# Local attention: the rounded part of the gated outputs by a second product on Pool, and the banded blocks' queries loaded two blocks ahead

## The chip, the core and the metric

The kernel runs on one core of a Trainium2 chip. A core has five engines that each take their own instructions in order: PE (TensorE, matrix products), DVE (VectorE), ACT (ScalarE), POOL (GpSimd) and SP (SyncE, which issues most of the DMA transfers here). They wait for one another by semaphores. The metric is the device time of one execution, in microseconds (us); lower is better.

## The reference

The reference is a two-layer backbone over 2048 latent tokens (a grid of 32 rows by 64 columns) of width 1024, with 256 context tokens beside them. Each layer normalises and modulates its input, projects it, runs two branches, multiplies each branch by its own gate, and projects the concatenation back into the residual:

```python
for layer in range(DEPTH):
    h = modulated_norm(x, norm_g[layer], shift[:, None], scale[:, None])
    p = jnp.matmul(h, w_in[layer])
    if layer % 2 == 0:
        y, y_ctx = even_mixer(p, p_ctx, ...)
    else:
        y, y_ctx = odd_mixer(p, p_ctx, ...)
    x = x + gate[:, None] * jnp.matmul(y, w_out[layer])
```

The change lies mostly in the second layer's mixer, whose two branches are local attention, each with 8 query heads of 64:

```python
y_w = windowed_gqa(q_w, k_w, v_w, kc_w, vc_w, sink)
y_n = neighbourhood_attention(q_n, k_n, v_n, kc_n, vc_n, rpb)
y = jnp.concatenate([y_w * jax.nn.silu(wg), y_n * jax.nn.silu(ng)], axis=-1)
```

Both also attend to the 256 context tokens. The banded branch has a sink logit and shares its two key heads among four query heads each; the neighbourhood branch adds a learned bias (`rpb`) by relative position.

## The kernel before

Products are taken in pieces: a float is split into a rounded part `hi` (in the type fp32r) and the rest `lo = y - hi`, and a matrix product is made of several products of such parts. So whatever is to be multiplied later is stored twice, as `hi` and as `lo`.

Layer 1's local attention is one sequence of blocks of four units each. It goes over four head pairs (`hp` 0 to 3); in each pair stand four banded blocks of 128 queries by 8 heads (`w`, `window(qt)`) and then four neighbourhood blocks of 512 queries by 2 heads (`n`, `nat_block(hp, qb)`): `"wwwwnnnn"`. The banded blocks are numbered through here, w0 to w15, four to a pair. That makes 32 blocks and 128 units. A unit forms scores for two heads at a time (L1493 and L1499 on PE), a masked minimum on DVE (L1549, or L1642 to L1647 for neighbourhood blocks), exponentials on ACT (L1551, or L1644 to L1650), transposes of the probabilities on PE (L1512) whose results ACT (first head) and DVE (second head) copy to SBUF (`npT`, L1514), and the products with the values on PE (L1524).

PE's order there is written by hand as a software pipeline: step i issues the transposes of unit i+1 between the scores of unit i+3, then the values of unit i, and then the end of the block that unit i-1 closed. So the gate matmuls of a block's end stand right ahead of the first scores of the block two further on. The other engines' orders come from the scheduler's own simulated timeline, and each engine then holds to its order.

The end of a block is `attn_out`, also used by the two context blocks of layer 0, which makes 34 uses. Ahead of it `attn_norm` copies the result from PSUM to the tile `ao` on ACT (L1096; a ring of three buffers). `attn_out` loads the gate (`ggt`, L1104), broadcasts the reciprocal sums on PE (`apr`, L1108), forms gate by reciprocal on DVE (L1109), and then: POOL multiplies `ao` by the gate (L1111), ACT rounds that into `ahi` (L1113), POOL subtracts to make `alo` (L1114), and SP stores both (L1116, L1117) to `yU`, which the output projection of the layer reads after all blocks are done.

Loads: the first unit of a block has a `load`. A banded block's load is 512 KB of queries (`wq1`, L1535, a ring of two buffers) and two halves of 128 KB (`wq2`, L1538, a ring of four); in the profile both are called `wq`. A neighbourhood block loads `nq1` and `nq2` (L1614, L1617). The loop calls the load of the next block when the second unit of a block gives its scores, so queries are loaded one block ahead:

```python
if su:
    if su.k == 1 and loaded < len(firsts):
        units[firsts[loaded]].load()
        loaded += 1
```

At the start of each head pair, its keys and values (L1600 to L1606) and its bias tables are made as well. For each of the pair's two heads, three pieces of bias are loaded by SP in several small transfers each (`raw`, L1589, three buffers), and POOL subtracts each from the mask to make a part of the table `tb` (L1590). The two heads' tables are read by the neighbourhood blocks behind the pair's four banded blocks.

Of the kernel before, what the change touches and what calls it, by code (L numbers as in the profile page):

```python
# [11 lines left out]
F32R = mybir.dt.float32r  # L12
AF = mybir.ActivationFunctionType
ALU = mybir.AluOpType
# [3 lines left out]
P = 128  # L18
# [16 lines left out]
def flow_kernel(tc, I, C, out):  # L35
    nc = tc.nc
    with ExitStack() as ctx:
        kern(ctx, tc, nc, I, C, out)


def kern(ctx, tc, nc, I, C, out):
    cp = ctx.enter_context(tc.tile_pool(name="cp", bufs=1))
    dr = ctx.enter_context(tc.tile_pool(name="dr", bufs=1, space=DRAM))
    V, S, G, T = nc.vector, nc.scalar, nc.gpsimd, nc.tensor
# [198 lines left out]
    class Proj:  # L243
# [6 lines left out]
        def __init__(self, layer, rg, hp, sb, lp, ps, npt, mms):  # L250

            self.layer, self.rg, self.hp, self.sb, self.lp, self.ps, self.npt = layer, rg, hp, sb, lp, ps, npt
            self.mms = [m for m in mms for _ in range(m[2])]
            self.nm = 0
            self.junk = sb, "sq"
            self.gains = {}
# [842 lines left out]
    def attn_out(A, D, order, parts):  # L1099


        gt = A.gt("ggt")
        for sl, g, _ in parts:
            nc.sync.dma_start(gt[sl], g)  # L1104
        pr = A.t("apr")
        for u in range(8):
            c = order(u)
            T.matmul(pr[64 * (u % 2):64 * (u % 2) + 64, u // 2, :], D["den"][:, c:c + 1].to_broadcast([P, 64]), ident, start=True, stop=True, skip_group_check=True)  # L1108
        V.scalar_tensor_tensor(out=gt, in0=pr, scalar=0.5, in1=gt, op0=ALU.mult, op1=ALU.mult)  # L1109
        y = D["o"]  # L1110
        G.tensor_tensor(out=y, in0=y, in1=gt, op=ALU.mult)  # L1111
        hi, lo = A.hl("ahi", F32R), A.hl("alo", F32R)
        S.copy(hi, y)  # L1113
        G.tensor_tensor(out=lo, in0=y, in1=hi.bitcast(F32), op=ALU.subtract)  # L1114
        for sl, _, st in parts:
            nc.sync.dma_start(st(0), hi[sl].bitcast(F32))  # L1116
            nc.sync.dma_start(st(1), lo[sl].bitcast(F32))  # L1117

    def by_head(t):
        return t.rearrange("f (b d) t -> d (f b) t", b=2)  # L1120
# [40 lines left out]
    with stS as st:  # L1161
# [33 lines left out]
        with ExitStack() as s2:  # L1195
# [16 lines left out]
            aw = []  # L1212
# [212 lines left out]
    for g in range(3):  # L1425
# [9 lines left out]
        if g == 2:  # L1435
            stX.close()
            aw = stA.enter_context(tc.tile_pool(name="aw", bufs=1, **L))
# [14 lines left out]
    with ExitStack() as st:  # L1452
        sb = st.enter_context(tc.tile_pool(name="at1", bufs=1, **Rt))
        ps = st.enter_context(tc.tile_pool(name="ats1", bufs=1, space=PSUM, **Rt))
        A = K()
# [19 lines left out]
        def probs():  # L1475
            return sb.tile([P, 896], F32, tag="np", name="np", bufs=7)

        class Unit:


            def __init__(self, B, k, qk, cols, kts, soft):
                self.B, self.k, self.qk, self.cols, self.kts, self.soft = B, k, qk, cols, kts, soft
                self.load = self.end = self.S_then = self.V_then = None
                self.last = False

            def scores(self):

# [41 lines left out]
        def window(qt):  # L1529
            tok = slice(qt * P, qt * P + P)  # L1530
            B = {"v": lambda: wvt}

            def load():
                q1 = aw.tile([P, 8, P], F32R, tag="wq1", name="wq1", bufs=2)
                nc.sync.dma_start(q1.bitcast(F32), qk1[0:8, :, tok].rearrange("h p t -> p h t"))  # L1535
                q2 = A.q2("wq2", F32R)
                for s in range(2):
                    nc.sync.dma_start(q2[64 * s:64 * s + 64].bitcast(F32), qk1[4 * s:4 * s + 4, 0:64, tok].rearrange("h p t -> p h t"))  # L1538
                B["q"] = q1, q2
                B["den"] = sb.tile([P, 8], F32, tag="gden", name="gden", bufs=3)  # L1540
                B["mx"] = sb.tile([P, 8], F32, tag="gmx", name="gmx", bufs=3)

            lo, hi = max(qt - 1, 0), min(qt + 1, 15)
            nl = (hi - lo + 1) * P
            m = wm[:, 640:1152] if qt == 0 else wm[:, 0:256 + nl]

            def soft(g, kv, s):
                h, p, mx, den = 4 * kv + g, probs(), B["mx"], B["den"]
                V.tensor_tensor_reduce(out=p[:, :256 + nl], in0=s[:, 256:512 + nl], in1=m, scale=1.0, scalar=sk[:, h:h + 1],  # L1549
                                       op0=ALU.add, op1=ALU.min, accum_out=mx[:, h:h + 1])  # L1550
                S.activation(p[:, :256 + nl], p[:, :256 + nl], AF.Exp, bias=mx[:, h:h + 1], scale=-1.0, accum_out=den[:, h:h + 1])  # L1551
                if g == 3 and kv == 1:
                    es = sb.tile([P, 8], F32, tag="ges", name="ges", bufs=2)
                    V.tensor_tensor(out=es, in0=mx, in1=sk, op=ALU.subtract)
                    S.activation(es, es, AF.Exp)
                    V.tensor_tensor(out=den, in0=den, in1=es, op=ALU.add)
                return p

            def end():
                store = [lambda t, kv=kv: by_head(yU[t, 0:4])[:, 4 * kv:4 * kv + 4, tok] for kv in range(2)]  # L1560
                attn_out(A, B, lambda u: 4 * (u % 2) + u // 2, [(slice(64 * kv, 64 * kv + 64), by_head(g1[0:4])[:, 4 * kv:4 * kv + 4, tok], store[kv]) for kv in range(2)])

            def qk(g):
                q1, q2 = B["q"]
                return lambda kv: q1[:, 4 * kv + g, :], q2[:, g, :], wk1, wk2

            us = [Unit(B, g, lambda g=g: qk(g), [(256, 2048, 256, True), (512, lo * P, nl, True)], [16, 17] + list(range(lo, hi + 1)),
                       lambda kv, s, g=g: soft(g, kv, s)) for g in range(4)]
            us[0].load, us[3].end = load, end
            return us  # L1570

# [22 lines left out]
        def nat_keys(hp):  # L1594
            hs = slice(18 + 2 * hp, 20 + 2 * hp)
            k1 = sb.tile([P, 2, 2304], F32R, tag="nk1", name="nk1", bufs=1)
            k2 = sb.tile([P, 2304], F32R, tag="nk2", name="nk2", bufs=1)
            for s in range(2):
                r = slice(64 * s, 64 * s + 64)
                nc.sync.dma_start(k1[r].bitcast(F32), qk1[hs, 0:64].rearrange("h p t -> p h t"))  # L1600
                nc.sync.dma_start(k2[r].bitcast(F32), qk1[18 + 2 * hp + s, 64:P])
            heads["k", hp] = k1, k2

        def nat_values(hp):
            heads["v", hp] = vt = sb.tile([P, 18, P], F32, tag="nv", name="nv", bufs=1)
            nc.sync.dma_start(vt, v1n[:, :, hp * P:(hp + 1) * P].rearrange("t p d -> p t d"))  # L1606
# [74 lines left out]
        units, qt = [], 0  # L1681
        for hp in range(4):
            qb = 0
            for i, what in enumerate("wwwwnnnn"):
                if what == "w":
                    units += window(qt)
                    units[-1].last = qt == 15
                    qt += 1
                    if i < 2:
                        units[-1].S_then = (lambda hp=hp: nat_tables(hp)) if i else lambda hp=hp: nat_keys(hp)  # L1690
                    continue
                us = nat_block(hp, qb)
                qb += 1
                if qb == 4 and hp < 3:
                    us[3].V_then = lambda hp=hp: nat_values(hp + 1)
                units += us
        n = len(units)
        firsts = [i for i, u in enumerate(units) if u.load]
        units[firsts[0]].load()
        nat_values(0)  # L1700
        loaded = 1
        with tc.manual_schedule(engines={mybir.EngineType.PE}):
            for i in range(-3, n + 1):
                su = units[i + 3] if i + 3 < n else None
                sc = su.scores() if su else [None] * 3
                tr = units[i + 1].transposes() if 0 <= i + 1 < n else []
                tr += [None] * (4 - len(tr))
                for f in (tr[0], sc[0], tr[1], sc[1], tr[2], sc[2], tr[3]):
                    if f:
                        f()  # L1710
                if su:
                    if su.k == 1 and loaded < len(firsts):
                        units[firsts[loaded]].load()
                        loaded += 1
                    if su.S_then:
                        su.S_then()
                if 0 <= i < n:
                    units[i].values()
                    if units[i].V_then:
                        units[i].V_then()  # L1720
                if 0 <= i - 1 < n and units[i - 1].end:
                    units[i - 1].end()
                    if units[i - 1].last:
                        prepare()
# [182 lines left out]
```

## Time and profile before

| | |
|---|---|
| median of three runs | 4063.99 us (4061.94 to 4068.01) |
| profiled execution | 4068.84 us |
| its span on the core | 4067.10 us |
| mean clock granted to PE | 0.954 of full speed |
| PE, busy share of the span | 91% |
| DVE | 61% |
| ACT | 44% |
| POOL | 41% |

The profile is one execution, recorded instruction by instruction. A row of the timeline gives the start in us from the span's beginning, the length in us, the engine, the line of the kernel, the operation and the tiles it writes and reads; brackets behind it hold the time for which the engine stood idle ahead of the row, and what ended that time. The waits group such idle times by who waited at which line for whom. The chain of waits follows the work that ended last back from the end of a stretch. A row of the table by stretches gives busy time of each engine with its count of instructions, the clock granted to PE (PEclk, 1.00 is full speed), the mean busy share of the DMA engines and the GB/s moved. A group of instructions is shown with its count, its busy time and the mean of one in ns, and then the idle time ahead of its rows.

The layer-1 local attention runs from about 3230 to 3890 us of the span.

### The profile page before, as it was taken

Reading aid. Unit: us, or ns where it says so; the run is one execution under the profiler, and the core shown is the slowest. Engines: PE = TensorE matmul, PEld = TensorE weight load, DVE = VectorE, ACT = ScalarE, POOL = GpSimd, SP = SyncE. Lnnn points to the kernel's source line nnn. Section 1 sums busy time; section 2 is a strip of 40 time slices with the busy share of each in tenths; the row PEclk is TensorE's granted clock in tenths of the full one; section 3 lists DMA queues with packets and bytes.
Section 4 is the critical chain, followed back from the end, with each engine's and each line's share of the span. In section 5 each row is a group of like instructions: output and inputs, shape, how many; then the busy total and the mean of one; then the engine's idle time right before and its main releaser. Section 6 shows DMA issues by size and latency. Waiting matters only on the chain.

```text
span 4067.1 us, 57048 instructions
## 1 busy us (share of the span) xinstructions
PE 3687.4 (91%) x20080; PEld 2634.0 (65%) x20080; DVE 2475.5 (61%) x4464; ACT 1794.6 (44%) x3460; POOL 1669.6 (41%) x1420
## 2 busy tenths in 40 slices
PE   6799889998959988899988989999998999989999
PEld 2588767656734443444444647777877877877887
DVE  6754852627769875688775528377158166666632
ACT  4554643425435543455443334343233265665610
POOL 1544542221456665576666555443344211121210
PEclk9899989999969998999998999999999999999999
DMA  6443445465474433343325435465466366265455
GB/s 189 102 137 120 131 121 139 126 240 186 141 211 130 134 115 134 95 136 122 96 103 174 127 109 162 144 178 155 131 192 162 118 161 140 82 145 126 121 156 173
DMA packets 525825, 576.14 MB, mean 142 GB/s; under 512 B 70790, under 2 KB 361920, under 8 KB 521442
## 3 DMA queue, kind: packets, MB, share of 16 engines
q1 hardware_dynamic: 516834, 547.25, 46.2%
q0 software_dynamic: 8704, 25.24, 1.6%
q8 instruction: 158, 2.59, 0.3%
q14 instruction: 129, 1.06, 0.1%
HBM read 383.73 MB, written 188.57 MB: 141 GB/s over the span
## 4 chain that ended last, share of the span: by engine, by line
PE 32%; DVE 6%; DMA 5%; issue 4%; POOL 2%; ACT 2%; SPq 1%; ACTq 0%; POOLq 0%; DVEq 0%
PE pso L215 7%; PE psB L215 4%; PE npt L1512 4%; PE no L1524 3%; PE psA L215 3%; PE po L950 2%; PE ns L1493 2%; DMA raw<-rpb 2%; PE ns L1499 1%; DMA wraw<-in_w_in_dram 1%; PE pS L929 1%; POOL wlo L237 1%; PE pS L930 1%; PE pm L887 1%; DMA wraw<-in_w_out_dram 1%
## 5 line engine op out<-in xcount | busy, mean ns | idle before, releaser
L237 POOL TENSOR_TENSOR wlo<-wraw,whi 128x512 fp32r<-128x512 f32 x368 | 488.5, 1343 | 872.3 <-ACT whi L236 600.2
L942 POOL TENSOR_TENSOR pacc<-pacc,Pt 128x512 f32<-128x512 f32 x448 | 609.0, 1378 | 314.4 <-ACT Pt L931 311.6
L215 PE MATMUL psB<-hT,whi 128*128 128x512 f32 (+1 forms) x2560 | 662.1, 348 | 19.6 <-DVE bo L333 7.4
L215 PE MATMUL psA<-whi,hT 128*128 128x512 f32 (+1 forms) x1952 | 569.9, 373 | 22.7 <-DVE hT L301 6.9
L931 ACT ACTIVATE Pt<-pS 128x512 f32<-128x512 f32 x576 | 336.0, 598 | 407.4 <-PE pS L930 396.4
L215 PEld LDWEIGHTS psB<-hT,whi 128*128 128x128 f32 x2560 | 447.1, 192 | 98.6 <-issue 16.5
L888 DVE TENSOR_REDUCE mx<-pm 128x1 f32<-128x512 f32 (+1 forms) x640 | 388.1, 630 | 151.6 <-PE pm L887 148.9
L215 PE MATMUL psB<-hT,wlo 128*128 128x512 f32 (+1 forms) x1280 | 438.6, 348 | 2.6 <-POOL wlo L237 2.5
L215 PEld LDWEIGHTS psA<-whi,hT 128*128 128x128 f32 x1952 | 355.7, 193 | 91.4 <-DVE hT L301 10.4
L215 PE MATMUL pso<-whi,oy 128*128 128x512 f32 x1088 | 346.5, 397 | 18.6 <-DMA oy<-yT 10.5
L215 PE MATMUL psA<-wlo,hT 128*128 128x512 f32 (+1 forms) x976 | 355.3, 369 | 1.3 <-POOL wlo L237 1.2
L929 PE MATMUL pS<-Q,K 128*128 128x512 f32 x576 | 341.2, 592 | 6.1 <-ACT Pt L931 5.7
L236 ACT CAST whi<-wraw 128x512 fp32r<-128x512 f32 x368 | 221.9, 618 | 268.3 <-DMA wraw<-in_w_in_dram 131.6
L887 PE MATMUL pm<-K,Q 128*128 128x512 f32 (+1 forms) x640 | 252.4, 422 | 77.3 <-DVE mx L888 58.1
L950 PE MATMUL po<-Pt,V 128*64 128x512 f32 x1152 | 291.8, 629 | 0.0
L1512 PE MATMUL npt<-ident,np 128*128 128x128 f32 x1488 | 262.2, 286 | 27.5 <-ACT npT L1514 25.5
L215 PEld LDWEIGHTS psB<-hT,wlo 128*128 128x128 f32 x1280 | 244.1, 191 | 39.0 <-POOL wlo L237 5.5
L215 PEld LDWEIGHTS pso<-whi,oy 128*128 128x128 f32 x1088 | 207.0, 191 | 71.0 <-ACT whi L236 9.9
L929 PEld LDWEIGHTS pS<-Q,K 128*128 128x128 f32 x576 | 114.2, 198 | 206.7 <-issue 145.6
L930 PE MATMUL pS<-Q,K 65*128 65x512 f32 x576 | 239.2, 415 | 6.2 <-DMA Q<-mr 6.2
L887 PEld LDWEIGHTS pm<-K,Q 128*128 128x128 f32 x640 | 133.2, 208 | 134.3 <-DVE mx L888 86.9
L1512 PEld LDWEIGHTS npt<-ident,np 128*128 128x128 f32 x1488 | 172.1, 142 | 73.4 <-ACT npT L1514 35.6
(334 smaller groups left out, 6784.4 us busy)
## 6 DMA issues: line engine op xcount, KB each, us to landing
wraw<-in_w_in_dram SPq DMA_DIRECT2D x312, 256.0 KB
oy<-yT SPq DMA_DIRECT2D x72, 512.0 KB
qk<-tq SPq DMA_DIRECT2D x68, 512.0 KB
fA<-fev SPq DMA_DIRECT2D x64, 256.0 KB
hxb<-XA SPq DMA_DIRECT2D x64, 256.0 KB
hfb<-fA SPq DMA_DIRECT2D x64, 256.0 KB
XC<-hevc POOLq DMA_DIRECT2D x64, 256.0 KB, 2.4
hdi<-XC SPq DMA_DIRECT2D x64, 256.0 KB
```

The lines of the kernel that those rows point to most:

```text
L215: T.matmul(ps, a(x, kt), b(y, kt), start=(kt == 0 and n == 0), stop=(kt == 7 and n == 2))
L236: S.copy(hi, w)
L237: G.tensor_tensor(out=lo, in0=w, in1=hi.bitcast(F32), op=ALU.subtract)
L887: T.matmul(pm[:, :n], q1[:, h, qt * P:(qt + 1) * P], K1[hp // 2][:, c0:c0 + n], start=True, stop=True)
L888: V.tensor_reduce(out=mx[:, u, c:c + 1], in_=pm[:, :n], axis=AX.X, op=ALU.max)
L929: T.matmul(s, K1[kv][:, kt * P:(kt + 1) * P], q1[:, h, :], start=True, stop=False)
L930: T.matmul(s, K2[kv][:, kt * P:(kt + 1) * P], q2[:, h, :], start=False, stop=True)
L931: S.activation(pt[:, h, :], s, AF.Exp)
L942: (G if e else V).tensor_tensor(out=acc[e][:, h], in0=acc[e][:, h], in1=p[:, h], op=ALU.add)
L950: T.matmul(po[64 * h:64 * h + 64, :], vt[:, kt, kv * 64:kv * 64 + 64], p[:, h, :], start=(kt == 0), stop=(kt == 17))
L1512: T.transpose(pt[:, i, :], self.p[h][:, (i0 + i) * P:(i0 + i + 1) * P], ident)
L1524: T.matmul(B["po"][64 * h:64 * h + 64, self.k, :], vt[:, kt, 64 * h:64 * h + 64], self.pT[h, i // 4][:, i % 4, :], start=(i == 0), stop=(i ...
```

## The change

There are two parts. In `attn_out` the rounded part is no longer a copy by ACT from the product, but a product of its own: POOL multiplies `ao` by the gate twice, once into `ahi` in the rounded type and once in place in full, and then subtracts. And a banded block's queries are loaded two blocks ahead: the ring `wq1` has three buffers, each banded block's first unit is marked `far`, and at a block's second unit all loads are made up to the next block, and to the one behind that if the next one still to be loaded is `far`.

```diff
@@ attn_out
         y = D["o"]
+        hi, lo = A.hl("ahi", F32R), A.hl("alo", F32R)
+        G.tensor_tensor(out=hi, in0=y, in1=gt, op=ALU.mult)
         G.tensor_tensor(out=y, in0=y, in1=gt, op=ALU.mult)
-        hi, lo = A.hl("ahi", F32R), A.hl("alo", F32R)
-        S.copy(hi, y)
         G.tensor_tensor(out=lo, in0=y, in1=hi.bitcast(F32), op=ALU.subtract)
@@ class Unit
-                self.last = False
+                self.last = self.far = False
@@ window
-                q1 = aw.tile([P, 8, P], F32R, tag="wq1", name="wq1", bufs=2)
+                q1 = aw.tile([P, 8, P], F32R, tag="wq1", name="wq1", bufs=3)
@@ the sequence of blocks
                     units[-1].last = qt == 15
+                    units[-4].far = True
...
-        firsts = [i for i, u in enumerate(units) if u.load]
-        units[firsts[0]].load()
+        firsts = [u for u in units if u.load]
+        firsts[0].load()
         nat_values(0)
-        loaded = 1
+        loaded, block = 1, -1
...
-                    if su.k == 1 and loaded < len(firsts):
-                        units[firsts[loaded]].load()
-                        loaded += 1
+                    if su.k == 1:
+                        block += 1
+                        while loaded < len(firsts) and loaded <= block + 1 + firsts[loaded].far:
+                            firsts[loaded].load()
+                            loaded += 1
```

What becomes of the engines' orders is shown at three places. The first is ACT at the start of the second head pair (`hp` 1), where `ahi_29636` is the rounded part of the last neighbourhood block of the pair before, `ges` closes a banded block's sums, `npT` are copies of transposed probabilities and `np` are exponentials. Before:

```order
L1555 ACTIVATE ges_29598<-ges_29598 128x8
L1514 COPY npT_29649<-npt_29644 128x512
L1514 COPY npT_29664<-npt_29662 128x128
L1113 CAST ahi_29636<-ao_29560 128x512
L1551 ACTIVATE np_29670,gden_29495<-np_29670,gmx_29496 128x640
L1551 ACTIVATE np_29673,gden_29495<-np_29673,gmx_29496 128x640
L1514 COPY npT_29697<-npt_29692 128x512
```

And of the change, the same place (buffer numbers are shifted by a few):

```order
L1555 ACTIVATE ges_29605<-ges_29605 128x8
L1514 COPY npT_29656<-npt_29651 128x512
L1514 COPY npT_29671<-npt_29669 128x128
L1551 ACTIVATE np_29677,gden_29228<-np_29677,gmx_29229 128x640
L1551 ACTIVATE np_29680,gden_29228<-np_29680,gmx_29229 128x640
L1514 COPY npT_29704<-npt_29699 128x512
```

The cast is gone, and nothing else has moved; over the local attention ACT loses its casts and keeps its order.

The second place is POOL at the same time. `alo_29391` belongs to the third neighbourhood block, `tb_29857` is the table of the pair's second head, and `ao_29560` is the last neighbourhood block's result. Before:

```order
L1111 TENSOR_TENSOR ao_29306<-ao_29306,ggt_29377 128x512
L1114 TENSOR_TENSOR alo_29391<-ao_29306,ahi_29390 128x512
L1590 TENSOR_TENSOR tb_29857<-nmask_27455,raw_29860 128x512
L1590 TENSOR_TENSOR tb_29857<-nmask_27455,raw_29864 128x512
L1590 TENSOR_TENSOR tb_29857<-nmask_27455,raw_29872 128x448
L1111 TENSOR_TENSOR ao_29560<-ao_29560,ggt_29623 128x512
L1114 TENSOR_TENSOR alo_29637<-ao_29560,ahi_29636 128x512
```

And of the change:

```order
L1590 TENSOR_TENSOR tb_29864<-nmask_27455,raw_29867 128x512
L1590 TENSOR_TENSOR tb_29864<-nmask_27455,raw_29871 128x512
L1590 TENSOR_TENSOR tb_29864<-nmask_27455,raw_29879 128x448
L1112 TENSOR_TENSOR ahi_29642<-ao_29567,ggt_29630 128x512
L1113 TENSOR_TENSOR ao_29567<-ao_29567,ggt_29630 128x512
L1114 TENSOR_TENSOR alo_29643<-ao_29567,ahi_29642 128x512
```

The products still stand behind the second head's three tables; there are two of them now, and the subtraction no longer has ACT ahead of it.

The third place is SP in the first head pair, where `wq1_27654` is the load of the third banded block (w2), among the table loads `raw`. Before:

```order
L1589 DMA raw_27767<-rpb_93 64x2x64
L1589 DMA raw_27775<-rpb_93 64x7x64
L1535 DMA wq1_27654<-qk1_89 128x8x128
L1589 DMA raw_27775<-rpb_93 64x7x64
L1538 DMA wq2_27919<-qk1_89 64x4x128 x2
L1614 DMA nq1_28146<-qk1_89 128x2x512
L1617 DMA nq2_28148<-qk1_89 64x512 x2
```

And of the change, where `wq1_27661` is the fourth banded block's load (w3):

```order
L1589 DMA raw_27774<-rpb_93 64x5x64
L1589 DMA raw_27774<-rpb_93 64x64
L1535 DMA wq1_27661<-qk1_89 128x8x128
L1589 DMA raw_27774<-rpb_93 64x2x64
L1589 DMA raw_27782<-rpb_93 64x7x64 x2
L1614 DMA nq1_28146<-qk1_89 128x2x512
L1617 DMA nq2_28148<-qk1_89 64x512 x2
```

The third block's load has left this place for one ahead of all table loads, beside the first two blocks' loads, and the fourth block's stands here instead. At the later pairs it is the same by one block: the load among the table loads is that of the pair's third banded block before (w6 at `hp` 1), and that of the fourth (w7) now.

The scheduler also puts some rows of layer 0 (about 640 to 960 us) and the first rows of the last projection in another order on PE, DVE and ACT.

## The prediction

> **What bounds the kernel now.** I read the page first (TensorE, PE, is busy 91% of the span, so only its waits and its clock are to be gained), then the waits of layer 1's attention, 3230 to 3900 us, where nearly all of the edit works.
>
> ```profile
> engine line waited for: us in total, times, longest us
> ...
> POOL tb L1590 <- DMA raw<-rpb: 117.5, 14, 58.0
> ...
> ACT ahi L1113 <- POOL ao L1111: 33.6, 14, 10.1
> ...
> PE npt L1512 <- ACT npT L1514: 25.5, 6, 9.0
> ...
> PE ns L1493 <- DMA wq<-qk: 5.7, 1, 5.7
> ```
>
> PE loses 25.5 us to ACT's copies of transposed probabilities, nearly all of it in three waits, and 5.7 us once to a load of a banded block's queries. ACT itself waits 33.6 us for POOL's gated product, 10.1 the longest. The chain of waits of 3395 to 3450, the second head pair's start, joins the two:
>
> ```profile
> 3402.88 19.35 DMA raw<-rpb
> ...
> 3424.28 4.02 DMA raw<-rpb
> 3428.44 1.12 POOL tb L1590
> 3429.56 1.23 POOL ao L1111
> ...
> 3431.33 1.73 ACT np L1551 x4
> 3433.06 0.48 ACT npT L1514
> 3433.58 0.47 PE npt L1512
> ```
>
> The rows of ACT, then POOL, then PE at that place (start, us, what; in brackets the idle time and what ended it) say what stands behind what:
>
> ```profile
> 3421.79 0.27 ACT L1514 COPY npT<-npt 128x128 f32<-128x128 f32 x1 [0.56 <-PE npt L1512]
> 3430.81 0.62 ACT L1113 CAST ahi<-ao 128x512 fp32r<-128x512 f32 x1 [8.75 <-POOL ao L1111]
> ...
> 3428.43 1.13 POOL L1590 TENSOR_TENSOR tb<-nmask,raw 128x448 f32<-128x448 f32 x1 [1.17 <-DMA raw<-rpb]
> ...
> 3433.58 0.47 PE L1512 MATMUL npt<-ident,np 128*128 128x128 f32 x1 [7.68 <-ACT npT L1514]
> ```
>
> POOL's product for the last neighbourhood block stands behind the second head's three tables, which wait for DMA. ACT takes its work in order: its cast waits 8.75 us, the exponentials (L1551) queue behind it, and PE stops 7.68 us for lack of probabilities. The stop also costs clock. The stretches (length, busy time of each engine, granted clock, DMA share) show it, 640 to 700 first, which is used further down:
>
> ```profile
> core 0: us, PE busy (x) PEld busy (x) DVE busy (x) ACT busy (x) POOL busy (x), PEclk, DMA share, GB/s
> 640.00:700.00 60.00, 60.00 (x329) 45.41 (x328) 14.71 (x35) 16.43 (x38) 15.36 (x12) 1.00 0.42 118
> 900.00:940.00 40.00, 26.98 (x126) 21.22 (x124) 39.58 (x27) 14.18 (x12) 11.96 (x5) 0.83 0.45 145
> 3278.50:3302.75 24.25, 18.55 (x172) 14.88 (x170) 12.19 (x29) 11.26 (x28) 9.82 (x8) 0.86 0.90 208
> 3302.75:3318.55 15.80, 15.80 (x173) 12.84 (x170) 11.35 (x29) 11.00 (x28) 2.56 (x2) 1.00 0.62 147
> 3418.93:3444.58 25.65, 17.96 (x172) 14.62 (x170) 11.54 (x29) 10.94 (x28) 6.16 (x5) 0.80 0.87 194
> 3444.58:3460.33 15.75, 15.75 (x173) 12.87 (x171) 11.34 (x29) 10.95 (x28) 2.56 (x2) 1.00 0.60 125
> 3576.50:3604.15 27.65, 18.64 (x172) 15.10 (x170) 11.56 (x29) 10.96 (x28) 6.16 (x5) 0.81 0.87 187
> 3604.15:3619.95 15.80, 15.80 (x173) 12.86 (x170) 11.39 (x29) 10.99 (x28) 2.55 (x2) 1.00 0.49 119
> 3736.06:3761.86 25.80, 18.02 (x172) 14.72 (x170) 11.49 (x29) 10.90 (x28) 6.15 (x5) 0.80 0.68 179
> 3761.86:3777.66 15.80, 15.80 (x173) 12.84 (x171) 11.46 (x29) 11.14 (x28) 2.56 (x2) 1.00 0.37 93
> 3433.50:3437.00 3.50, 3.42 (x24) 2.87 (x25) 0.29 (x1) 1.82 (x6) 0.00 (x0) 0.50 1.25 224
> ```
>
> The other rows are pairs: one banded block from the gate matmuls of one block's end (apr, L1108) to those of the next, at a head pair's start, and behind it the next block of the same pair. Both do 172 or 173 matmuls; undisturbed, PE is busy all of 15.8 us. The difference, idle time and lost clock together, is what a stop costs.
>
> The Trainium skill, "TensorE: Matmul & The Clock Gate", "HAM oscillation", says that a gap of PE over about 3.4 us brings half clock for a window of about that length; the row of 3433.50 (a clock of 0.50 for 3.5 us, right behind the stop) agrees, and by that rule the gain is the 40.2 below and not the idle time of 5.7 + 25.5 = 31.2.
>
> **The change part by part.** *The cast leaves ACT.* At the three later head pairs nothing between exponentials and copies waits for POOL any more. Worth 25.65 − 15.75 = 9.90, 27.65 − 15.80 = 11.85 and 25.80 − 15.80 = 10.00: **31.75 us**.
>
> What is late next? ACT's copy of `no` to `ao` (L1096), which now waits for POOL's subtraction of three blocks before. With three buffers the one of the last neighbourhood block goes to the third banded block behind it (w6). POOL comes free for its gated products at 3429.56 (chain); three products of 1.28 end at about 3433.4. The w6 copy comes just ahead of its gate matmuls, in the time of after at 3460.33 + 15.8 − 9.9, about 3466: some 30 us of slack.
>
> *The queries come a block earlier.* The issues of SP (SyncE, its DMA queue), then the load in the chain of waits, the last table of the first head pair and its first reader:
>
> ```profile
> 3021.61 2.00 SPq L1535 DMA_DIRECT2D wq<-qk  x2
> ...
> 3259.64 19.88 SPq L1589 DMA_DIRECT2D raw<-rpb  x9
> 3279.70 1.01 SPq L1535 DMA_DIRECT2D wq<-qk  x1
> 3431.14 0.80 SPq L1535 DMA_DIRECT2D wq<-qk  x1
> ...
> 3279.70 6.01 DMA wq<-qk
> ...
> 3296.71 1.14 POOL L1590 TENSOR_TENSOR tb<-nmask,raw 128x448 f32<-128x448 f32 x1 [1.08 <-DMA raw<-rpb]
> ...
> 3322.90 0.74 DVE L1647 CUSTOM_DVE_ANT_0 np<-ns,tb,nmx 128x512 f32<-128x512 f32 x1
> ```
>
> At the first head pair the third block's queries stand behind nine table loads, which hold SP for 19.88 us; they land 6.01 us after issue, and PE stops 5.70. In the order of after they stand ahead of those loads. Worth 24.25 − 15.80 = **8.45 us**. Late next is the fourth block's load, which takes the old one's place: issued by about 3283, landed by 3289, used behind the second gate matmuls at 3302.75 − 8.45 = 3294.3: 5 us of slack. That load and half of the neighbourhood queries now also stand ahead of the second head's table loads. The last table is there at 3297.85 (3296.71 + 1.14); 6 us more, one such load, makes 3304, and the first reader comes at 3322.90 − 8.45 = 3314.5: 10 us of slack.
>
> At the later pairs this half matters through the other: w6's queries are issued at 3431.14 and land at about 3437.2; with 9.90 us gone they would be wanted behind 3444.58 − 9.90 = 3434.7, 2.5 us too late. Here w7's take that place and are wanted behind 3460.33 − 9.90 = 3450.4, 13 us after landing.
>
> *The second product.* Each block end has POOL do three products instead of two.
>
> ```profile
> L1111 POOL TENSOR_TENSOR ao<-ao,ggt 128x512 f32<-128x512 f32 x32 | 40.8, 1276 | 337.0 <-ACT npT L1514 103.6 <-DVE gden L1094 87.5 <-DVE nden L1094 49.8
> L1113 ACT CAST ahi<-ao 128x512 fp32r<-128x512 f32 x32 | 19.8, 617 | 33.9 <-POOL ao L1111 33.6
> L1651 DVE TENSOR_TENSOR nden<-nmx x32: 159/160/1228, 3325.0 to 3879.2; 128x1 f32<-128x1 f32 x32
> 3402.43 1.22 DVE L1651 TENSOR_TENSOR nden<-nmx 128x1 f32<-128x1 f32 x1
> 3887.83 0.50 PE L215 MATMUL pso<-whi,oy 128*128 128x512 f32 x1 [0.85 <-DVE ggt L1109]
> ```
>
> 34 × 1.276 = 43.4 us of POOL, hidden: POOL is busy 2.56 of 15.80 us in a block, and the stores that follow have no reader for blocks. The cover is gone only at the end, where POOL also prepares weights (wlo, L237): at most 1.3 us by this row, taken as 0, since PE's 0.85 us at 3887.83 goes to DVE. ACT saves 34 × 0.617 = 21.0 us, beside PE's work: 0.
>
> The third row gives DVE's smallest sum: 159 or 160 ns, and 1228 ns at the worst. One of 1.22 us (3402.43) stands beside POOL's tables. So more POOL time can stretch DVE. If each of the four pairs paid 1.07 twice, it were 8.5 us; from below it is 0, as PE is busy throughout the undisturbed blocks. I take **+1**, near the lower end, because DVE has over 4 us of room in a block.
>
> The Trainium skill, "GPSIMD Engine Reference", § 8 "Key points", speaks against the change: elementwise work is about twice as fast on VectorE, and the two engines contend where a VectorE instruction has two SBUF inputs. L1651 has two and shows 160 against 1228 ns; by that rule at every block the sum would be the 34 us worse that stands among the rivals.
>
> *The third buffer* adds a load of 512 KB to the two issued at 3021.61, ahead of the value tiles (v1w) and the next weights. PE is in projections there, with weights read earlier: 0 to 3 us, the length of one issue (2.00 for two); I take **+1**. *Layer 0* has the same function twice (the context blocks, in 640 to 700, where PE is busy 60.00 of 60.00), worth 0; but the scheduler also puts some PE, DVE and ACT rows of about 640 to 960 us in another order. PE has 13 us idle in 900 to 940, at a clock of 0.83. Some 60% of that idle time, either way: ±8, taken as 0, as no row says which way.
>
> **Sum**: 31.75 + 8.45 = 40.2 gained, 2 lost, 38.2. The profiled execution took 4068.84 (span 4067.10), so 4030.6; it lay 4.85 above the median of the three runs (4063.99), which makes **4025.8, so 4026**. What a measurement can tell from no change is about 0.2%, 8.1 us: 4055.9 to 4072.1.
>
> **Rivals.**
> - *The later pairs' queries are still late.* If SP reaches the row late, as at the first pair where nine loads held it 19.88 us, PE stops again and the clock drops: 2 to 6 us at three places, about +10, 4036. Against it are the 13 us of slack.
> - *Layer 0 moves.* ±8 us: 4018 or 4034. The moved rows speak for it; the 60.00 of 60.00 and that PE's own sums are the same, against.
> - *POOL beside DVE at every block.* 32 × 1.07 = 34 us if PE waits for each: 4060. For: the 1228 ns. Against: the median of 160 ns, with two POOL products in each block already.
> - *The change doesn't do what it says.* ACT waits for POOL at L1096 in place of L1113 and the exponentials queue as before: 4064. It decides if POOL is held over 30 us longer than shown; the 58.0 us among the waits for tables is the first pair's start.
> - *Slower: SP stands at a query load.* The new load waits until PE is through with the block whose buffer it takes. Stood there early, SP would hold tables, gates and neighbourhood queries behind it. Held for one banded block at each pair, 4 × 15.8 = 63 us: 4026 + 63 = 4089. It decides once the hold is longer than the 13 us of slack. Against it: the row at 3431.14 goes out in 0.80 us, and the buffer then wanted (w4's) is done with before 3418.93.
>
> **How the numbers follow.** Forecast 0.68 (its own range 4018 to 4036), queries late 0.12, layer 0 0.10, POOL and DVE 0.03, no effect 0.04, slower 0.03. From the first three comes a range of 4014 (layer 0's gain and nothing lost elsewhere) to 4046 (queries late together with layer 0's loss). Faster by over 0.2%: the first four, 0.93 (the 4060 of the fourth is its upper end; half of it is 4043); same 0.04; slower 0.03.
>
> **What would show it.** Right: four blocks at the head pairs' starts of 15.8 to 17 us, clock 1.00 there; no wait of PE for ACT's npT over 2 us; POOL still waiting for tables as long as before, with nobody behind it; L1590 followed by L1112, L1113, L1114. Wrong: a wait of ACT at L1096 for POOL, or of PE for wq, at a head pair; L1651's median off 160 ns; 640 to 960 us longer or shorter by several us.

## The result, and the profile after

The changed kernel took 4018.77 us (median of 4 runs, 4013.32 to 4026.27), the kernel before 4062.97 in the same set (4060.39 to 4068.01). The ratio is 0.9893, with a 95% interval of 0.9879 to 0.9906: about 43.5 us faster, between 38 and 49. Two further sets, called 2 and 3 below, gave 0.990 (0.9887 to 0.9914) and 0.9885 (0.987 to 0.990); every ratio is to the kernel before in the same set. The profiled execution of the changed kernel took 4015.50 us, with a span of 4013.7.

First the four places where the prediction had lengths of 24 to 28 us. These are the same stretches in the changed kernel's trace, from the gate matmuls (L1108) of one block to those of the next, with the granted clock behind the busy times; the second row is the block after the first:

```profile
core 0: us, PE busy (x) PEld busy (x) DVE busy (x) ACT busy (x) POOL busy (x), PEclk, DMA share, GB/s
3265.39:3281.18 15.79, 15.79 (x172) 12.83 (x170) 11.45 (x29) 10.52 (x27) 6.23 (x5) 1.00 0.97 209
3281.18:3297.34 16.16, 16.02 (x172) 12.89 (x170) 11.71 (x29) 10.48 (x27) 8.73 (x7) 1.00 0.63 136
3397.72:3413.53 15.81, 15.81 (x173) 12.85 (x171) 11.47 (x29) 10.58 (x27) 7.50 (x6) 1.00 0.98 222
3545.44:3561.24 15.80, 15.80 (x172) 12.83 (x170) 11.46 (x29) 10.53 (x27) 6.83 (x6) 1.00 0.95 210
3693.17:3708.92 15.75, 15.75 (x173) 12.84 (x171) 11.41 (x29) 10.47 (x27) 7.51 (x6) 1.00 0.93 218
```

The clock is full in all of them, and PE is busy throughout but for 0.14 us of the second row. The waits of the local attention (3230 to 3850 us), which answer to the first rows of the prediction:

```profile
POOL tb L1590 <- DMA raw<-rpb: 63.1, 13, 15.1
POOL tb L1590 <- PE npt L1512: 59.5, 1, 59.5
...
PE npt L1512 <- ACT npT L1514: 0.5, 2, 0.3
```

POOL waits for its tables as long as before (117.5 us then, 63.1 + 59.5 now; of the longest wait the trace names another releaser), but PE's 25.5 us for ACT's copies are 0.5, and it waits for `wq` nowhere any more. At the second head pair POOL's rows and then ACT's show why:

```profile
3401.30 1.28 POOL L1590 TENSOR_TENSOR tb<-nmask,raw 128x512 f32<-128x512 f32 x1 [13.82 <-DMA raw<-rpb]
...
3406.85 1.15 POOL L1590 TENSOR_TENSOR tb<-nmask,raw 128x448 f32<-128x448 f32 x1 [1.66 <-DMA raw<-rpb]
3407.95 1.28 POOL L1112 TENSOR_TENSOR ahi<-ao,ggt 128x512 fp32r<-128x512 f32 x1
3409.31 1.28 POOL L1113 TENSOR_TENSOR ao<-ao,ggt 128x512 f32<-128x512 f32 x1
3410.67 1.28 POOL L1114 TENSOR_TENSOR alo<-ao,ahi 128x512 fp32r<-128x512 f32 x1
```

```profile
3400.59 0.27 ACT L1514 COPY npT<-npt 128x128 f32<-128x128 f32 x1 [0.56 <-PE npt L1512]
3401.95 0.83 ACT L1551 ACTIVATE np<-np,gmx 128x640 f32<-128x640 f32 x1 [1.09 <-DVE gmx L1549]
...
3410.21 0.56 ACT L1096 COPY ao<-no 128x512 f32<-128x512 f32 x1
```

POOL still stands 13.82 us for the table load, and the gated products still stand behind the tables. ACT, though, goes from its copy to the next exponential in a little over a microsecond, and its copy to `ao` (L1096) waits for nothing.

### The profile page after: what moved, and what is told of

The parts are those of the page before. It is cut to its first block, busy times and chain, and to the rows that moved or that the text cites. A ratio compares the mean times of both kernels' runs of the same rounds, so it can differ in the third digit from the quotient of the medians.

```text
span 4013.7 us, 57053 instructions
## 1 busy us (share of the span) xinstructions
PE 3669.8 (91%) x20080; PEld 2618.8 (65%) x20080; DVE 2470.2 (62%) x4464; ACT 1777.2 (44%) x3426; POOL 1715.1 (43%) x1454
## 4 chain that ended last, share of the span: by engine, by line
PE 33%; DVE 7%; issue 4%; DMA 4%; ACT 2%; POOL 2%; SPq 0%; ACTq 0%; POOLq 0%; DVEq 0%
PE pso L215 7%; PE npt L1512 4%; PE psB L215 4%; PE psA L215 4%; PE no L1524 4%; PE po L950 2%; PE ns L1493 2%; PE ns L1499 2%; PE pS L929 1%; POOL wlo L237 1%; DMA wraw<-in_w_out_dram 1%; DMA wraw<-in_w_in_dram 1%; PE pS L930 1%; DVE tq L207 1%; PE pm L887 1%
## 5 line engine op out<-in xcount | busy, mean ns | idle before, releaser
L215 PE MATMUL psB<-hT,whi 128*128 128x512 f32 (+1 forms) x2560 | 665.1, 349 | 17.4 <-DVE bo L333 7.4
L215 PE MATMUL psA<-whi,hT 128*128 128x512 f32 (+1 forms) x1952 | 568.7, 372 | 22.4 <-DVE hT L301 6.5
L215 PEld LDWEIGHTS psB<-hT,whi 128*128 128x128 f32 x2560 | 448.1, 192 | 95.9 <-issue 15.0
L215 PE MATMUL psB<-hT,wlo 128*128 128x512 f32 (+1 forms) x1280 | 438.1, 347 | 3.4 <-POOL wlo L237 3.4
L215 PEld LDWEIGHTS psA<-whi,hT 128*128 128x128 f32 x1952 | 354.5, 192 | 91.9 <-DVE hT L301 10.3
L215 PE MATMUL pso<-whi,oy 128*128 128x512 f32 x1088 | 344.2, 395 | 16.2 <-DMA oy<-yT 7.8
L215 PE MATMUL psA<-wlo,hT 128*128 128x512 f32 (+1 forms) x976 | 354.5, 368 | 1.0 <-POOL wlo L237 0.8
L887 PE MATMUL pm<-K,Q 128*128 128x512 f32 (+1 forms) x640 | 249.9, 419 | 78.6 <-DVE mx L888 57.8
L215 PEld LDWEIGHTS psB<-hT,wlo 128*128 128x128 f32 x1280 | 244.4, 191 | 38.6 <-POOL wlo L237 6.1
L215 PEld LDWEIGHTS pso<-whi,oy 128*128 128x128 f32 x1088 | 205.5, 189 | 67.3 <-ACT whi L236 9.1
L887 PEld LDWEIGHTS pm<-K,Q 128*128 128x128 f32 x640 | 132.2, 207 | 135.5 <-DVE mx L888 86.7
L215 PE MATMUL pso<-wlo,oy 128*128 128x512 f32 x544 | 214.2, 395 | 5.0 <-POOL wlo L237 5.0
```

What stands on the lines that cost most here:

```text
L215: T.matmul(ps, a(x, kt), b(y, kt), start=(kt == 0 and n == 0), stop=(kt == 7 and n == 2))
L887: T.matmul(pm[:, :n], q1[:, h, qt * P:(qt + 1) * P], K1[hp // 2][:, c0:c0 + n], start=True, stop=True)
```

## The experiments

All lengths named below are those of the stretches above. The attention's length runs from the start of the first scores (L1493) to the end of the last gate matmuls (L1108); the expectations measured to the start of these, which makes their figures about 1 us smaller.

### The second product alone

```diff
 (the kernel before, with)
+        G.tensor_tensor(out=hi, in0=y, in1=gt, op=ALU.mult)
         G.tensor_tensor(out=y, in0=y, in1=gt, op=ALU.mult)
-        S.copy(hi, y)
```

> The second product alone, with two query buffers and loads one block ahead as before. Theory (two causes that cover one another): ACT no longer waits at the later head pairs, but the third banded block's queries, issued as before about 3431 and landing 6 us later, are then wanted some 2.5 us before they land, so PE waits for wq at the three later pairs instead: first banded block behind each pair's start 18 to 22 us long in place of 25.65, 27.65, 25.80, the first head pair's as before (24.25, wait for wq 5.7). Gain 14 to 26 us, a time of 4037 to 4049. Rival (the cast alone): no wait for wq at the later pairs, 15.8 us there, gain 31.75 and a time near 4031.

Measured: 4040.11 us, ratio 0.9949 (0.9937 to 0.9961), about 21 us faster. PE's wait for `wq`, the rows that end it at the four pairs, and the lengths there (each followed, for the first three pairs, by the undisturbed block behind it):

```profile
PE ns L1493 <- DMA wq<-qk: 13.8, 4, 7.0
```

```profile
3277.66 0.88 PE L1493 MATMUL ns<-wk,wq 128*128 128x256 f32 x2 [7.02 <-DMA wq<-qk]
...
3430.66 0.53 PE L1493 MATMUL ns<-wk,wq 128*128 128x256 f32 x2 [2.42 <-DMA wq<-qk]
...
3581.91 0.53 PE L1493 MATMUL ns<-wk,wq 128*128 128x256 f32 x2 [3.30 <-DMA wq<-qk]
...
3732.50 0.53 PE L1493 MATMUL ns<-wk,wq 128*128 128x256 f32 x2 [1.10 <-DMA wq<-qk]
```

```profile
3269.01:3294.41 25.40, 18.38 (x173) 14.72 (x171) 11.46 (x29) 10.65 (x27) 11.02 (x9) 0.80 0.92 206
3294.41:3310.43 16.02, 16.02 (x173) 12.89 (x170) 11.28 (x29) 10.49 (x27) 3.84 (x3) 1.00 0.59 147
3426.61:3445.02 18.41, 15.99 (x173) 12.86 (x171) 11.36 (x29) 10.44 (x27) 3.82 (x3) 1.00 0.87 201
3445.02:3460.82 15.80, 15.80 (x173) 12.84 (x171) 11.47 (x29) 10.54 (x27) 3.85 (x3) 1.00 0.41 103
3576.98:3597.87 20.89, 17.59 (x172) 14.04 (x170) 11.42 (x29) 10.61 (x27) 4.25 (x4) 0.92 0.75 179
3597.87:3613.63 15.76, 15.76 (x172) 12.86 (x170) 11.34 (x29) 10.42 (x27) 3.85 (x3) 1.00 0.41 104
3729.76:3746.90 17.14, 16.04 (x172) 12.88 (x170) 11.47 (x29) 10.54 (x27) 3.84 (x3) 1.00 0.58 158
```

ACT's stop is gone at the later pairs, and the query load takes its place one block further on, at 2.42, 3.30 and 1.10 us: the theory, with a price of 2.6 + 5.1 + 1.3 = 9.0 us of the 31.75 (the last length, 17.14, lies under its 18 to 22). The first pair keeps its wait. The rival, the cast alone, falls.

### The queries alone

```diff
 (the changed kernel, with)
-        G.tensor_tensor(out=hi, in0=y, in1=gt, op=ALU.mult)
         G.tensor_tensor(out=y, in0=y, in1=gt, op=ALU.mult)
+        S.copy(hi, y)
```

> Three query buffers and loads two blocks ahead, the cast still on ACT. Theory: only the first head pair's wait for wq goes (24.25 to about 15.8, gain 8.45); the later pairs keep ACT's wait for POOL of 8 to 10 us and lengths of 25 to 28 us. A time of about 4054 to 4056. Rival (the early loads do the work): the later pairs' stops go as well, 4023.

Measured: 4059.36 us, ratio 0.9997 (0.9987 to 1.0008). That is no gain, and neither the theory's 8.45 nor the rival's. The lengths at the four pairs, with the block behind the first:

```profile
3271.33:3298.31 26.98, 18.63 (x173) 15.08 (x171) 11.55 (x29) 10.97 (x28) 9.85 (x8) 0.81 0.84 179
3298.31:3314.11 15.80, 15.80 (x173) 12.84 (x171) 11.34 (x29) 11.01 (x28) 2.56 (x2) 1.00 0.72 163
3414.49:3439.57 25.08, 17.51 (x173) 14.24 (x171) 11.54 (x29) 10.95 (x28) 6.16 (x5) 0.86 0.89 201
3571.47:3596.88 25.41, 17.25 (x173) 13.96 (x171) 11.55 (x29) 10.96 (x28) 6.17 (x5) 0.87 0.90 200
3728.80:3755.45 26.65, 18.72 (x172) 15.21 (x170) 11.49 (x29) 10.90 (x28) 6.16 (x5) 0.81 0.65 168
```

The first pair is not shorter than before (24.25), although PE waits for `wq` nowhere. What it waits for stands in the rows of POOL, ACT and PE there:

```profile
3281.51 1.13 POOL L1590 TENSOR_TENSOR tb<-nmask,raw 128x448 f32<-128x448 f32 x1 [1.55 <-DMA raw<-rpb]
3282.59 1.26 POOL L1111 TENSOR_TENSOR ao<-ao,ggt 128x512 f32<-128x512 f32 x1
```

```profile
3283.88 0.62 ACT L1113 CAST ahi<-ao 128x512 fp32r<-128x512 f32 x1 [9.43 <-POOL ao L1111]
```

```profile
3286.66 0.47 PE L1512 MATMUL npt<-ident,np 128*128 128x128 f32 x1 [8.35 <-ACT npT L1514]
```

This is the later pairs' stop, at the first pair: the first banded block's product stands behind the first head's tables, the cast waits 9.43 us for it, and PE 8.35. In the kernel before, PE was already waiting for `wq` at that time, so the trace had only the load to show.

### The third buffer alone

```diff
-                q1 = aw.tile([P, 8, P], F32R, tag="wq1", name="wq1", bufs=2)
+                q1 = aw.tile([P, 8, P], F32R, tag="wq1", name="wq1", bufs=3)
```

> The third query buffer alone; each load still made one block ahead in the program. Theory: the scheduler may only let a load go a little earlier; no stop goes, a time of 4060 to 4066 (the term of +1 for a third early load is not in it). Rival (it is the buffer, not the order of the loads, that frees the first pair's wait): 4055.

Measured: 4059.00 us, ratio 0.9992 (0.9982 to 1.0003); lengths at the pairs of 23.56, 24.76, 27.13 and 25.77 us. The time shows nothing, neither the gain of the rival nor the +1 of the prediction. But the rival's mechanism is there: PE's wait for `wq` at the first pair went by the buffer alone, and the cast's stop (6.21 us of ACT, 5.12 of PE there) came out from under it here too. SP's rows of the query loads say how, first in this kernel and then in the changed one (the first three loads together, w0 to w2, and then the seventh, w6):

```profile
3011.39 4.38 SPq L1535 DMA_DIRECT2D wq<-qk  x3
...
3304.15 0.37 SPq L1535 DMA_DIRECT2D wq<-qk  x1
```

```profile
3010.48 5.46 SPq L1535 DMA_DIRECT2D wq<-qk  x3
...
3305.38 0.58 SPq L1535 DMA_DIRECT2D wq<-qk  x1
```

In the kernel before, w2 went out at 3279.70 and w6 at 3431.14. With a third buffer both are issued over 100 us earlier, at the places of the changed kernel, although the program still calls each load one block ahead: "a little earlier" was wrong. So the earlier loads that the changed kernel lives on may be the work of the buffer, and that the new loop is needed beside it is not shown: the second product with the third buffer and the old loop was not run.

### The kernel before once more

> The kernel before once more, unchanged, for a second profile of it. Theory: the local attention's lengths repeat within 1 us, and what differs ahead of it (between 0 and 3230 us of the span, where the two profiles of before and after lie 11.9 us apart) differs between two executions of the same kernel by several us too. Rival (the change moves the layers ahead of the attention): this profile reaches the attention within 2 us of the first profile of before.

Its profiled execution took 4055.49 us, 13.35 less than the first. Its lengths at the pairs:

```profile
3264.25:3289.25 25.00, 18.38 (x172) 14.71 (x170) 11.46 (x29) 11.27 (x28) 9.87 (x8) 0.86 0.94 209
3405.46:3431.39 25.93, 17.55 (x172) 14.25 (x170) 11.55 (x29) 10.97 (x28) 6.17 (x5) 0.80 0.89 197
3563.32:3590.35 27.03, 18.77 (x173) 15.22 (x171) 11.56 (x29) 10.97 (x28) 6.16 (x5) 0.81 0.87 189
3722.27:3748.43 26.16, 17.76 (x172) 14.47 (x170) 11.49 (x29) 10.91 (x28) 6.16 (x5) 0.80 0.67 176
```

They repeat within 0.8 us. The stages ahead do not: the attention starts at 3240.27 us here and at 3253.26 in the first profile, with the same instructions in the same order. The rival falls.

### The changed kernel again, twice

> The changed kernel once more, unchanged, for a narrower interval and a second profile. Theory: lengths of 15.7 to 16.2 us at all four head pairs' starts again, a gain in the local attention of 40 us and of nothing elsewhere beyond what two executions differ by, so a ratio of 0.989 to 0.991. Rival (the layers ahead of the attention gain too, some 4 to 12 us): 0.986 to 0.989, with this profile reaching the attention ahead of both profiles of before.

> The changed kernel a third time, unchanged, beside the two above on the same chip. Theory: the attention takes 590 to 593 us again and begins between 3238 and 3254; ratio to before 0.989 to 0.991.

Measured: 4016.54 us (4015.32 to 4019.16) and 4014.03 us (4005.73 to 4016.41), at the ratios given above. The lengths at the pairs' starts are 15.79, 15.80, 15.79, 15.75 and 15.80, 15.80, 15.80, 15.75 us, and the attention begins at 3240.20 and 3237.72. The last of these and the ratio of 0.9885 lie just outside what was expected of the third profile (3238, 0.989).

### One more product on POOL

```diff
         G.tensor_tensor(out=hi, in0=y, in1=gt, op=ALU.mult)
+        G.tensor_tensor(out=lo, in0=y, in1=gt, op=ALU.mult)
         G.tensor_tensor(out=y, in0=y, in1=gt, op=ALU.mult)
```

> The changed kernel with one more gated product on POOL at each block end (into the tile of the rest, which the subtraction then overwrites): 34 x 1.28 = 43 us more of POOL. Theory: hidden, since POOL has over 10 us free in a block of 15.8 and the stores have no reader for blocks: within 3 us of the changed kernel, lengths of 15.8 unchanged, DVE's L1651 median at 160 ns. Rival (POOL's time beside DVE is paid at every block): 1.07 to 1.28 us a block, 34 to 43 us more, about 4055 to 4060.

Measured: 4023.71 us, ratio 0.9918 (0.9903 to 0.9934), some 7 us behind the changed kernel's 0.990 in the same set. The attention took 591.7 us, against 592.3 to 594.4 of the changed kernel's three profiles, with lengths of 15.79, 15.81, 15.80 and 15.74 at the pairs; it began at 3247.98. So the cost of POOL's time in the attention is nothing, as the theory has it, and the 7 us lie elsewhere, against its "within 3 us". The groups (busy time, mean ns of one) of the added product and of DVE's smallest sum, one line further down in this kernel, and then that sum in the changed kernel:

```profile
L1113 POOL TENSOR_TENSOR alo<-ao,ggt 128x512 fp32r<-128x512 f32 x32 | 40.9, 1278 | 0.0
...
L1652 DVE TENSOR_TENSOR nden<-nmx 128x1 f32<-128x1 f32 x32 | 13.6, 425 | 13.9 <-ACT np L1651 13.8
```

```profile
L1651 DVE TENSOR_TENSOR nden<-nmx 128x1 f32<-128x1 f32 x32 | 10.3, 320 | 15.7 <-ACT np L1650 15.6
```

DVE does get slower beside POOL, by 3.3 us over 32 sums; PE pays none of it. The median of the sum is 160 ns here, 160 in the kernel before and 159 in the changed one, and its 32 rows took 10.3 us before as well: the second product of the change costs it nothing.

### Other engines for the same products

Three kernels keep the queries two blocks ahead and share the end of a block out otherwise. On POOL, a copy in place of the second product:

```diff
-        G.tensor_tensor(out=hi, in0=y, in1=gt, op=ALU.mult)
         G.tensor_tensor(out=y, in0=y, in1=gt, op=ALU.mult)
+        G.tensor_copy(hi, y)
```

> The changed kernel, but the rounded part is a copy of the product made by POOL and not a second product. Theory: what counts is that ACT has no work behind POOL's tables, so it takes the same time as the changed kernel within 4 us. Rival (the second product as such matters, for a copy of POOL takes several us or it stops DVE): over 10 us slower than the changed kernel.

Both products on DVE:

```diff
-        G.tensor_tensor(out=hi, in0=y, in1=gt, op=ALU.mult)
-        G.tensor_tensor(out=y, in0=y, in1=gt, op=ALU.mult)
+        V.tensor_tensor(out=hi, in0=y, in1=gt, op=ALU.mult)
+        V.tensor_tensor(out=y, in0=y, in1=gt, op=ALU.mult)
```

> The changed kernel, but both gated products on DVE (VectorE) and only the subtraction on POOL. Theory: DVE has over 4 us free in a block, and two products take some 0.6 us each, so the time is that of the changed kernel within 4 us, and the lengths of 15.8 stay. Rival (the page's rule that elementwise work belongs on VectorE): a gain of some us over the changed kernel, 4010 or less; or, as the products stand ahead of DVE's npT copies and minima, 1 us lost at each of 32 blocks, 4050.

One product on DVE, and the cast back on ACT:

```diff
-        G.tensor_tensor(out=hi, in0=y, in1=gt, op=ALU.mult)
-        G.tensor_tensor(out=y, in0=y, in1=gt, op=ALU.mult)
+        V.tensor_tensor(out=y, in0=y, in1=gt, op=ALU.mult)
+        S.copy(hi, y)
```

> Three query buffers and loads two blocks ahead as in the changed kernel, one gated product on DVE, the cast back on ACT, and the subtraction on POOL. Theory: what stopped PE was POOL's place behind the tables, not ACT's cast as such; with the product on DVE the cast waits for nothing long, the four lengths at the head pairs' starts are 15.8 to 17 us and the attention from its first scores to its last gate matmuls takes 590 to 597 us, as in the changed kernel (591.2). Rival (ACT's work itself is what counts, or the cast still meets a late POOL): 25 us again at the pairs' starts, 630.

Measured, with the changed kernel in the first row for each set:

| set | kernel | median us | ratio to before | attention, us | attention begins at |
|---|---|---|---|---|---|
| 2 | changed | 4016.54 | 0.9900 (0.9887 to 0.9914) | 593.6 | 3240.20 |
| 2 | copy on POOL | 4027.42 | 0.9924 (0.9910 to 0.9938) | 592.5 | 3253.57 |
| 2 | products on DVE | 4027.18 | 0.9921 (0.9905 to 0.9937) | 595.7 | 3238.62 |
| 3 | changed | 4014.03 | 0.9885 (0.9870 to 0.9900) | 594.4 | 3237.72 |
| 3 | product on DVE, cast on ACT | 4028.26 | 0.9928 (0.9915 to 0.9940) | 593.9 | 3250.12 |
| 3 | copy on POOL | 4030.39 | 0.9927 (0.9915 to 0.9940) | 592.1 | 3255.66 |

The attention is within 3.5 us of the changed kernel's in all of them, against 633.7 and 633.3 us before. The product on DVE with the cast back on ACT is the telling one: there the cast is on ACT as it ever was, and no stop is left, because the product ahead of it is not on POOL behind the tables. So it was the place in POOL's order, not ACT's 0.62 us. The products on DVE take 722 and 708 ns each and leave no stop either, but gain nothing. The times are another matter: "within 4 us" was expected of the copy on POOL and of the products on DVE, and both took over 10 us more. For the copy this is the rival's number but not its reason, since the copy takes 0.61 us and the attention is no longer. The Trainium skill, "GPSIMD Engine Reference", § 4.1 "Engine selection", has two-input elementwise work about twice as slow on GpSimd; 1.28 us against 0.71 to 0.72 agrees, and it makes no time here, where PE sets the pace.

> The kernel with POOL's copy once more, unchanged. In the last set it took 10.9 us more than the changed kernel by the median, while its attention was as long (591.5 against 591.2 and 592.5); all of it lay ahead of the attention, which it reached at 3253.6. Theory A (executions of one kernel differ by that much ahead of the attention, as two profiles of before do, 3253.3 and 3240.3): the difference shrinks to under 6 us here. Theory B (the scheduler's other order in layer 0 costs it): again 8 to 14 us behind the changed kernel, and its profile reaches the attention at 3250 or later.

The copy on POOL is slower than the changed kernel by 10.9 and then 16.4 us, and begins its attention 12 to 18 us later in both of its profiles; the kernel with the cast on ACT is slower by 14.2 and begins 9 to 12 us later. So the difference repeats, as theory B has it (16.4 is more than its 8 to 14), and lies ahead of the attention. That the rows of layer 0 moved at 640 to 960 us cost it is not borne out. Two rows of PE stand between: the first product of layer 0's own attention (`pm`, L887), and the first of layer 1's input projection (`psA`, L215). They begin, in us of the span:

| kernel | `pm` | `psA` | from `pm` to `psA` |
|---|---|---|---|
| changed, three profiles | 1146.69, 1140.81, 1140.66 | 2433.48, 2426.34, 2426.17 | 1286.8, 1285.5, 1285.5 |
| copy on POOL, two profiles | 1146.48, 1141.73 | 2440.35, 2441.09 | 1293.9, 1299.4 |
| product on DVE, cast on ACT | 1139.63 | 2437.05 | 1297.4 |

At `pm` the copy on POOL lies within the changed kernel's own spread; most of what it loses, and most of the other kernel's loss, comes between the two rows, and there DVE, ACT and POOL also run some rows in another order than in the changed kernel (about 2100 to 2500 us). The kernels with a third product and with both products on DVE take 1295.8 and 1295.2 us there, so the third product's 7 us arise there as well. Which of the moved rows costs it was not tried. The products on DVE began their attention early in the profiled execution (which took 4016.09 us, the lowest of 4016.09 to 4031.67), so for that kernel the 10 us can't be placed as a whole.

## Why the prediction was right, and where it was not

The forecast was 4026 in a range of 4014 to 4046; 4018.77 lies inside it, and the gain is 43.5 us of 38.2 forecast. The ends of the range are 2 us wider than their own terms give: 4026 − 8 − 2 = 4016 and 4036 + 8 = 4044, which hold the time as well.

**The sum in the attention held.** It went from 633.7 and 633.3 us before to 592.3, 593.6 and 594.4: by the means, 633.5 − 593.4 = 40.1. The prediction had 40.2 gained and 1 lost there. Pair by pair, in the two profiles that came with the result: 24.25 − 15.79 = 8.46, 25.65 − 15.81 = 9.84, 27.65 − 15.80 = 11.85 and 25.80 − 15.75 = 10.05.

**The part of it on the first head pair was put down to the wrong half.** "The queries come a block earlier ... Worth 24.25 − 15.80 = 8.45" named the load as what stops PE there. The runs of one half each show two stops of about one length: with the load early and the cast kept, 26.98; with the cast gone and the load late, 25.40; only with both gone, 15.79. That the term of 8.45 came out at 8.46 is luck in so far: the reason given for it is worth nothing alone, and the other half, which was in the change for the later pairs, supplied the rest. What stood late next was the very stop that the prediction had found at the later pairs, and it did not look for it at the first, where POOL's tables also stand ahead of a block's products.

**Each half needs the other: wholly at the first pair, for a part at the later ones.** The latter was foreseen: queries "2.5 us too late" against 2.42, 3.30 and 1.10 us measured. By the profiled lengths at the later pairs, the second product alone gains 31.75 − 9.0 = 22.75 us, the queries alone 2.0 (25.08, 25.41 and 26.65 for 25.65, 27.65 and 25.80), both 31.7; over all four pairs the queries alone gain nothing and both gain 40.2.

**The added costs were nothing in the attention.** The +1 for POOL beside DVE: the blocks behind the stops are 15.8 us long as before, even with a third product, but for the one at the first pair, which is 16.16 in place of 15.80. The +1 for the third load is under what the runs can tell. Of the rivals, no wait of ACT for POOL at L1096 and none of PE for `wq` stands in the trace; SP waits at the query loads for 17.3 us in seven waits, less than the 37.7 in eight before. The ±8 for layer 0 came out near 0 up to 1147 us: its attention's first product begins between 1140.1 and 1146.9 in the four profiles with the order of before, and between 1140.7 and 1146.7 in the four with the changed one.

**The rest is what one execution is worth.** Against the profiled execution's forecast of 4030.6 the changed kernel's took 4015.5, 15.1 less. Of this 2.2 lie in the attention (41.4 between these two profiles, 39.2 forecast) and 12.9 ahead of it, where 1 was to be lost and 11.9 were gained. What was off is the base: the prediction took the profiled execution as 4.85 above the kernel's time. The same kernel reached its attention 13.0 us earlier in its second profile, and its medians in the later sets were 4060.17, 4058.89 and 4058.55. So the sum began from a slow start of the span. Whether the changed order ahead of the attention also brings a few us stays open. By the medians of sets 2 and 3 the gain is 42.4 and 44.5 us, 2 to 4 more than the attention's 40.1; the kernels with the order of before (the queries alone and the buffer alone among them) began their attention at 3253.26, 3240.27, 3246.65 and 3242.08, those with the changed one (the second product alone among them) at 3244.92, 3241.32, 3240.20 and 3237.72. From `pm` to `psA` it took 1288.7 to 1291.4 us with the order of before and 1285.5 to 1286.8 in the changed kernel, but 1290.2 with the second product alone, whose rows on DVE, ACT and POOL stand there in the changed order.

## What to carry to other kernels

An engine that takes its work in order can pass on a wait of its neighbour, as ACT's 8.75 us for POOL became 7.68 of PE: look for a short operation that sits between two engines and whose producer stands behind slow transfers, and move the operation or its producer, not the wait. Where one stop is removed, look at the same place for a second one that ended a little earlier; when two causes cover one another, each half alone may show nothing. Where a change gives a load both a buffer and an earlier place in the program, try the buffer alone first: here it moved the loads by itself. And a gain of a per cent is to be read stage by stage from landmarks in the trace, since the stages that the edit leaves alone can differ by as much between two executions.

## What the runs showed of the hardware

The run with the second product alone gives a scale for what a stop of PE costs. The lengths less the undisturbed 15.8 are 1.3 us for a stop of 1.10, 2.6 for 2.42, 5.1 for 3.30 (clock 0.92 over the block) and 9.6 for 7.02 (clock 0.80). Up to 2.42 us the price is little more than the stop; slow clock adds 1.8 us at 3.30 and 2.6 at 7.02. The Trainium skill, "TensorE: Matmul & The Clock Gate", "HAM oscillation", puts the limit at about 3.4 us; the stop of 3.30 lies just under it and already paid.

POOL's copy into the rounded type took 0.61 us, less than half of its 1.28 for the product, and as long as ACT's 0.62; in the attention it made no difference. The scheduler's order is not local to an edit: a change of a line or two in `attn_out`, which layer 0 uses twice, at about 655 and 683 us, moved rows of other engines' work up to 960 us, and for the copy on POOL also at 2100 to 2500 us, far from any use of it. There that kernel lost 7 to 14 us, more than any difference between these kernels within the attention; that the order is what costs it is likely but was not tried.
